# Contracting the ones products of squared rotary halves over 128 rows instead of 64

## The chip, the cores and the metric

The kernel runs on all eight cores of one Trainium2 chip. Each core works on its own share of the tokens and no core waits for another. The metric is the device time of the slowest core in microseconds (us). Executions of a program on all eight cores fall into two states. In the slow state the cores of one die, sometimes of both, show a lower granted TensorE clock than the others (0.83 against 0.99 in one run of the changed kernel, 3170.24 us). The dies are cores 0 to 3 and cores 4 to 7. PE is TensorE (matmuls), PEld its weight loads, DVE is VectorE, ACT is ScalarE, POOL is GpSimd.

## The reference, cut to what matters

```python
# multi-head latent attention, 16 heads, q and k have 128 plain and 64 rotary dimensions
q = apply_rope_tail(rmsnorm(q, q_norm_g[l]), cos, sin)      # norm over all 192
k = apply_rope_tail(rmsnorm(k, k_norm_g[l]), cos, sin)      # k_rope is shared by all heads
y_mla = causal_block_attention(q, k, v) @ w_mla_out[l]
```

The norm needs the sum of 192 squares per token. The kernel keeps dimensions on partitions (rows) and tokens on columns. So it forms these sums on TensorE, as products with a matrix of ones: 128 squared plain dimensions and 64 squared rotary dimensions.

## The kernel before

Two places multiply 64 rows of squares by ones. One is `krstat`, once for each of the 16 key groups of the key/value stage. The other is the unit `QS`, three times for each of the 16 heads of the head stage. `PS[b]` is bank b of the memory into which matmuls write; the latents are the compressed keys and values.

```python
def krstat(g):
    for bb in range(2):                       # one output column each
        mm(PS[BKV][:, 256 + bb:257 + bb], sqkr[0:64, bb * 128:(bb + 1) * 128], ones[0:64, 0:1], True, True,
           [Tsqkr, Tones], [TP[BKV]])
    cp(krss[:, 2 * g:2 * g + 2], PS[BKV][:, 256:258], [TP[BKV]], [Tkrss])

# key/value stage, one turn per key group (cut): 80 latent matmuls of 256 columns into banks 0 to 4,
# first those into bank 0; latents_out reads bank 0 first, on DVE
latents(g); squares(g + 2); kvstat(g); latents_out(g); xstat(g + 2); krstat(g)

def QS(t):
    off, n = QT[t]                            # n = 348, 348, 344
    p = fbank()
    mm(PS[p][:, 0:n], ones, sqn[:, 0:n], True, False, [Tones, Tsqn], [TP[p]])
    mm(PS[p][:, 0:n], ones[0:64, :], sqr[0:64, 0:n], False, True, [Tones, Tsqr], [TP[p]])
    rsq(rsqh[:, 0:n], PS[p][:, 0:n], 192.0, [TP[p]], [Trsqh])        # ACT: Ln, Exp
    ...                                                              # DVE: normalised q

# head stage, per key block (cut): scores, exponential, mask, product with v, running sums
mm(PS[b][:, o:o + n], Kn[hb][:, ks], Qn[hb][:, 128 + lo:128 + hi], True, False, ...)
mm(PS[b][:, o:o + n], krope[:, ks], Qr[hb][:, 128 + lo:128 + hi], False, True, ...)
act(PT[:, x, a:912], psum[:, z + a:z + 912], AF.Exp, ...)            # ACT
tt(PT[:, x, a:a + w], PT[:, x, a:a + w], mask[:, r, 0:w], ALU.mult, ...)                    # DVE, w = 130
mm(PS[b][:, o:o + hi - lo], Vh[hb][:, kb, :], PT[:, x, lo:hi], kb == 0, kb == last, ...)
tt(acc[:, z, a:912], acc[:, z, a:912], PT[:, x, a:912], ALU.add, ...)                       # DVE
```

The program orders each engine's instructions once, when it is built, by a modelled clock. On the chip every engine runs its own list in order and waits on semaphores.

Of the kernel before, what the change touches and what calls it, by code (L numbers as in the profile page):

```python
# [13 lines left out]
PE, ACT, DVE, POOL, SP = "tensor", "scalar", "vector", "gpsimd", "sync"  # L14
# [275 lines left out]
def build_program():  # L290
# [20 lines left out]
    PS = [psum[:, 512 * i:512 * i + 512] for i in range(8)]  # L311
    TP = [T("ps%d" % i, excl=True) for i in range(8)]
    S = Sched(nc)
# [58 lines left out]
    def width(ap):  # L372
        n = 1
        for d in ap.shape[1:]:
            n *= d
        return n

    def mm(out, lhsT, rhs, start, stop, reads, writes):
        S.add(PE, lambda e: e.matmul(out, lhsT=lhsT, rhs=rhs, start=start, stop=stop), reads, writes,  # L379
              cost=max(width(rhs) / 2400.0, 0.055) + 0.003)  # L380
# [9 lines left out]
    def stt(out, in0, scalar, in1, op0, op1, reads, writes):  # L390
        S.add(DVE, lambda e: e.scalar_tensor_tensor(out=out, in0=in0, scalar=scalar, in1=in1, op0=op0, op1=op1),  # L391
              reads, writes, cost=dcost(out, in0, in1))

    def tt(out, in0, in1, op, reads, writes):
        S.add(DVE, lambda e: e.tensor_tensor(out=out, in0=in0, in1=in1, op=op), reads, writes,  # L395
              cost=dcost(out, in0, in1))

    def ts(out, in0, s1, s2, op0, op1, reads, writes):
        c = dcost(out, in0)
        if s2 is None:  # L400
            S.add(DVE, lambda e: e.tensor_scalar(out=out, in0=in0, scalar1=s1, scalar2=None, op0=op0), reads, writes,  # L401
                  cost=c)
        else:
            S.add(DVE, lambda e: e.tensor_scalar(out=out, in0=in0, scalar1=s1, scalar2=s2, op0=op0, op1=op1),  # L404
                  reads, writes, cost=c)

    def cp(out, in_, reads, writes):
        S.add(DVE, lambda e: e.tensor_copy(out=out, in_=in_), reads, writes, cost=dcost(out, in_))  # L408
# [4 lines left out]
    def rsq(out, ssq, n, reads, writes):  # L413

        act(out, ssq, AF.Ln, reads, writes, scale=1.0 / n, bias=EPS)
        act(out, out, AF.Exp, writes, writes, scale=-0.5)
# [4 lines left out]
    ones, Tones = P0.tile([128], BF16, "ones")  # L421
# [102 lines left out]
    sqkr, Tsqkr = P1.tile([GW], BF16, "sqkr")  # L524
# [33 lines left out]

    S.add(DVE, lambda e: e.memset(ones, 1.0), writes=[Tones])  # L559
    S.add(DVE, lambda e: e.memset(krope[64:128, :], 0.0), writes=Tkr)  # L560
    INV2PI = 1.0 / (2.0 * math.pi)
    C1 = 6.28125
    C2 = 2.0 * math.pi - 6.28125
# [5 lines left out]
    for which, dst, Tdst in ((0, tS, TtS), (1, tC, TtC)):  # L569
        if which == 0:  # L570
            ts(rq, ang, INV2PI, None, ALU.mult, None, [Tang], [Trq])
        else:
            ts(rq, ang, INV2PI, 0.25, ALU.mult, ALU.add, [Tang], [Trq])
        cp(rn, rq, [Trq], [Trn])
# [24 lines left out]
    BST, BKV = 6, 5  # L599
# [46 lines left out]

    def krstat(g):
        for bb in range(2):
            mm(PS[BKV][:, 256 + bb:257 + bb], sqkr[0:64, bb * 128:(bb + 1) * 128], ones[0:64, 0:1], True, True,
               [Tsqkr, Tones], [TP[BKV]])  # L650
        cp(krss[:, 2 * g:2 * g + 2], PS[BKV][:, 256:258], [TP[BKV]], [Tkrss])

# [33 lines left out]
    for g in range(NG):  # L686
        if g + 1 < NG:
            make_u(g + 1)
        if g + 3 < NG:
            xload(g + 3)  # L690
        latents(g)
        if g + 2 < NG:
            squares(g + 2)
        kvstat(g)
        latents_out(g)
        if g + 2 < NG:
            xstat(g + 2)
        krstat(g)
        if g == 2:
            halo()  # L700
# [13 lines left out]
    def bank(n=5):  # L714
        b = bk[0] % n
        bk[0] += 1
        return b

    pend = []
    for i in range(6):  # L720
        wv, Tw = wget(("qlat", i))
        for t, (off, n) in enumerate(T3):
            p = bank()
# [43 lines left out]
    sqr, Tsqr = P4.tile([348], BF16, "sqr")  # L767
# [22 lines left out]
    Tgd = [T("gd%d" % i) for i in range(8)]  # L790
    for i_ in range(2):
        S.add(DVE, lambda e, i_=i_: e.memset(Qr[i_][64:128, :], 0.0), writes=[TQr[i_]])  # L792


    class Unit:
# [14 lines left out]
    def fbank():  # L810
        return cur[0]
# [66 lines left out]
    def prologue_units(h):  # L878
# [66 lines left out]
        def QS(t):  # L945
            off, n = QT[t]
            p = fbank()
            mm(PS[p][:, 0:n], ones, sqn[:, 0:n], True, False, [Tones, Tsqn], [TP[p]])
            mm(PS[p][:, 0:n], ones[0:64, :], sqr[0:64, 0:n], False, True, [Tones, Tsqr], [TP[p]])
            rsq(rsqh[:, 0:n], PS[p][:, 0:n], 192.0, [TP[p]], [Trsqh])  # L950

            stt(Qn[hb][:, off:off + n], qraw[:, 0:n], gqe, rsqh[:, 0:n], ALU.mult, ALU.mult,
                [Tqraw, Tgqe, Trsqh], [TQn[hb]])
            tt(Qr[hb][0:64, off:off + n], qr_[0:64, 0:n], rsqh[0:64, 0:n], ALU.mult, [Tqr_, Trsqh], [TQr[hb]])
# [24 lines left out]
        for t in range(3):  # L979
            qq += [Unit(U("q", QN, t), 0.87, ok=okk), Unit(U("q", QR, t), 0.87),  # L980
                   Unit(U("q", QS, t), 0.3, need=[Tsqn, Tsqr], strict=True)]
# [302 lines left out]
    while any(s.units for s in streams):  # L1284
# [19 lines left out]
        if best is None:  # L1304
            n = sum(len(x.pend) for x in streams)
# [17 lines left out]
    for c in range(16):  # L1323
        for key, dst, Td, bo in (("ga", sga, Tsga, 0), ("gb", sgb, Tsgb, 16)):
            w, Tw = wget((key, c))
            for t, (off, n) in enumerate(T3):
                p = bank(8)
# [36 lines left out]
    for c in range(16):  # L1364
        w, Tw = wget(("wo", c))
        for t, (off, n) in enumerate(T3):
            p = bank()
# [199 lines left out]
```

## Time and profile before

| | before |
|---|---|
| time, median of 4 runs | 2769.61 us (2767.91 to 2771.78) |
| matmuls busy, of the span | 95% |
| loads of 64 rows, of all weight loads | 80 of 18,722 |
| excess time at the 48 QS places | 9.8 us |
| period of a key group, median of 15 | 12.92 us |

Groups by form, core 1: weight loads and matmuls of 64 rows. After the bar stand busy us and mean ns of one, then idle us before them and what ended it.

```profile
L379 PEld LDWEIGHTS ps<-arena 128*128 128x128 bf16 x18642 | 1644.6, 98 | 1076.0 <-issue 232.6
L379 PEld LDWEIGHTS ps<-arena 64*128 64x128 bf16 x80 | 6.4, 93 | 24.2 <-issue 24.2
...
L379 PE MATMUL ps<-arena 64*128 64x348 bf16 x32 | 10.2, 318 | 0.0
L379 PE MATMUL ps<-arena 64*128 64x344 bf16 x16 | 5.1, 317 | 0.0
L379 PE MATMUL ps<-arena 64*128 64x1 bf16 x32 | 3.0, 160 | 9.3 <-ACT arena L384 9.3
```

A load of 64 rows takes about as long as one of 128 rows (93 and 98 ns). The idle time before them differs. Of the 24.2 us, 13.3 us stand before the 16 `krstat` pairs, which wait for ACT; 10.9 us stand before the 48 QS loads, 0.23 us each, against 0.06 us before a load of 128 rows.

The timeline around one QS, same core: start us, duration us, engine and instruction.

```profile
442.48 1.39 PE L379 MATMUL ps<-arena 128*128 128x390 bf16 x9
442.81 0.10 PEld L379 LDWEIGHTS ps<-arena 128*128 128x128 bf16 x1
443.21 0.09 PEld L379 LDWEIGHTS ps<-arena 64*128 64x128 bf16 x1 [0.30 <-issue]
443.46 0.28 PEld L379 LDWEIGHTS ps<-arena 128*128 128x128 bf16 x5 [0.16 <-issue]
```

The 64-row load is not pulled ahead of the running matmul as loads usually are. It comes at 443.21, and the next 128-row load comes a quarter of a microsecond later. The single matmuls start at 442.976 (128 rows), 443.218 (64 rows) and 443.469 (128 rows). These are steps of 242 and 251 ns, where 348 columns take 147 ns in a stream.

Worked out from the trace:

- **Excess** of a matmul: its start minus its predecessor's start, minus the predecessor's pace (columns/2.4 + 2.5 ns). That pace comes out of the trace of before, core 1: the median steps after 128, 256, 348, 390 and 512 columns are 56, 109, 147, 165 and 216 ns, where the formula gives 55.8, 109.2, 147.5, 165.0 and 215.8. It is sorted into QS places, places with a semaphore wait for DVE or ACT, and others, and averaged over the six cores of each run whose matmul records are complete.
- **Length of the head stage**: from weight load 2044 to weight load 9100, counted from 0 (the order of instructions is the same in both kernels, and weight-load records are complete; in e2 the same two loads), mean of eight cores. Where a 3.4 us window at half the granted clock fell into it (steps of 427 ns instead of 216 after 512 columns), half of that window is taken off. Most cores of one run then agree to 0.2 us, all to 0.5 us. The slowest core's time doesn't resolve this well: one core's start and end move by several us between runs.

### The profile page before, as it was taken

The numbers are of one execution on the slowest core, as the hardware profiler recorded it, in microseconds if no ns is written. First come the engines' busy times: TensorE is split into PE (matmuls) and PEld (weight loads), VectorE is DVE, ScalarE is ACT, GpSimd is POOL, SyncE is SP. The second block draws the span as 40 slices with busy tenths as digits, with TensorE's granted clock in tenths as the row PEclk, the third lists the DMA queues.
The fourth block names the chain that finished last, engine by engine and source line by source line (L and its number), as shares of the span: only waits on it lengthen the run. The fifth ranks groups of instructions, "written<-read, shape, count | busy, mean of one in ns | idle before, by whom it ended". The sixth has DMA issues, their size and how long they took to land.

```text
span 2770.5 us, 51821 instructions; the slowest of 8 cores (2758.7 to 2770.5 us)
## 1 busy us (share of the span) xinstructions
PE 2624.4 (95%) x18612; PEld 1652.4 (60%) x18722; DVE 1637.5 (59%) x3248; ACT 891.9 (32%) x1598; POOL 172.3 (6%) x300
## 2 busy tenths in 40 slices
PE   3899899999999999999999999999999999999997
PEld 2777555565565555555666666666646646655653
DVE  5774477878887888886111112247727745754762
ACT  3553366656656666664111112320000000000000
POOL 0000000000000000000000000001111011111100
PEclk9999899999999999999999999999999999999999
DMA  9552302020212020215444447444454444444445
GB/s 239 162 171 45 59 18 41 15 41 15 47 18 45 15 41 15 34 42 123 76 72 80 73 75 175 97 73 74 69 83 77 72 74 84 74 69 81 76 87 142
DMA packets 67113, 205.65 MB, mean 74 GB/s; under 512 B 7600, under 2 KB 7856, under 8 KB 66736
## 3 DMA queue, kind: packets, MB, share of 16 engines
q0 software_dynamic: 42624, 135.94, 29.7%
q1 hardware_dynamic: 24240, 66.38, 7.3%
q8 instruction: 157, 2.57, 0.4%
q14 instruction: 92, 0.75, 0.1%
HBM read 321.34 MB, written 14.78 MB: 121 GB/s over the span
## 4 chain that ended last, share of the span: by engine, by line
PE 80%; DVE 6%; issue 5%; ACT 4%; DMA 3%; SPq 1%; DVEq 0%; ACTq 0%; POOLq 0%
PE ps L379 80%; ACT arena L384 4%; DVE arena L395 3%; DMA outT<-arena 2%; DVE arena L391 2%; DVE arena L408 1%; DMA arena<-arena 1%; SPq L411 0%; DVE arena L401 0%; DMA arena<-wall 0%; DVEq L183 0%; ACTq L183 0%; DVE arena L404 0%; DVE arena L560 0%; DVE arena L792 0%
## 5 line engine op out<-in xcount | busy, mean ns | idle before, releaser
L379 PE MATMUL ps<-arena 128*128 128x390 bf16 (+10 forms) x18612 | 2624.4, 299 | 133.4 <-ACT arena L384 81.7
L379 PEld LDWEIGHTS ps<-arena 128*128 128x128 bf16 x18722 | 1652.4, 98 | 1104.9 <-issue 263.3
L395 DVE TENSOR_TENSOR arena<-ps,arena 128x390 f32<-128x390 f32 (+6 forms) x760 | 380.5, 508 | 830.8 <-PE ps L379 716.4
L395 DVE TENSOR_TENSOR arena<-arena 128x512 bf16<-128x512 bf16 (+20 forms) x1458 | 625.6, 474 | 95.6 <-ACT arena L384 69.2
L384 ACT ACTIVATE arena<-ps,arena 128x128 bf16<-128x128 f32 (+10 forms) x672 | 436.2, 672 | 478.0 <-PE ps L379 433.7
L384 ACT ACTIVATE arena<-arena 128x390 bf16<-128x390 f32 (+11 forms) x374 | 227.6, 636 | 898.7 <-DVE arena L391 788.5
L391 DVE SCALAR_TENSOR_TENSOR arena<-arena 128x256 bf16<-128x256 f32 (+8 forms) x583 | 419.7, 755 | 90.2 <-ACT arena L384 67.4
L384 ACT ACTIVATE arena<-ps 128x512 bf16<-128x512 f32 (+13 forms) x547 | 248.5, 472 | 375.3 <-PE ps L379 371.3
L411 POOL DMA_DIRECT2D arena<-wall x294 | 170.9, 582 | 2562.1 <-PE ps L379 2327.7
L408 DVE CAST arena<-ps 128x512 bf16<-128x512 f32 x128 | 87.9, 687 | 45.8 <-PE ps L379 44.4
L404 DVE TENSOR_SCALAR arena<-arena 128x1024 f32<-128x1024 f32 (+1 forms) x90 | 72.3, 803 | 2.6 <-ACT arena L384 2.5
L391 DVE SCALAR_TENSOR_TENSOR arena<-ps,arena 128x256 bf16<-128x256 f32 x64 | 26.5, 476 | 48.8 <-ACT arena L384 48.8
L408 DVE COPY arena<-ps 128x456 f32<-128x456 f32 (+2 forms) x64 | 27.1, 424 | 1.4 <-DVE arena L395 0.5
L401 DVE TENSOR_SCALAR arena<-arena 128x390 f32<-128x390 f32 (+7 forms) x36 | 20.5, 570 | 7.9 <-DMA arena<-arena 5.4
L384 ACT ACT_TABLE_LOAD x5 | 6.4, 1283 | 33.7 <-DVE arena L401 15.5
L395 DVE TENSOR_TENSOR arena<-arena,ps 128x390 bf16<-128x390 f32 (+1 forms) x24 | 12.3, 511 | 2.4 <-PE ps L379 1.5
L408 DVE COPY arena<-arena 128x6 f32<-128x6 f32 (+2 forms) x32 | 9.4, 293 | 2.0
L560 DVE MEMSET arena<- 64x4096 bf16 x1 | 3.5, 3472 | 0.9 <-issue 0.9
L408 DVE CAST arena<-arena 128x1028 f32<-128x1028 int32 (+1 forms) x5 | 3.5, 697 | 0.4
L792 DVE MEMSET arena<- 64x1040 bf16 x2 | 1.9, 925 | 0.4 <-issue 0.4
L559 DVE MEMSET arena<- 128x128 bf16 x1 | 0.2, 165 | 1.2 <-PEq L291 1.2
L411 POOL DMA_DIRECT2D arena<-wkvin x1 | 0.7, 664 | 0.9 <-POOLq L291 0.9
(5 smaller groups left out, 0.9 us busy)
## 6 DMA issues: line engine op xcount, KB each, us to landing
arena<-wall POOLq DMA_DIRECT2D x182, 512.0 KB, 5.8
arena<-xg SPq DMA_DIRECT2D x64, 512.0 KB, 5.2
arena<-wall POOLq DMA_DIRECT2D x64, 352.0 KB, 4.5
arena<-xo SPq DMA_DIRECT2D x16, 520.0 KB, 24.7
arena<-wall POOLq DMA_DIRECT2D x32, 256.0 KB, 3.8
outT<-arena SPq DMA_DIRECT2D x32, 256.0 KB, 3.0
arena<-wall POOLq DMA_DIRECT2D x16, 384.0 KB, 5.1
att_d<-arena SPq DMA_DIRECT2D x16, 260.0 KB, 2.1
```

Source lines behind the costliest of these rows:

```text
L379: S.add(PE, lambda e: e.matmul(out, lhsT=lhsT, rhs=rhs, start=start, stop=stop), reads, writes, cost=max(width(rhs) / 2400.0, 0.055) + 0.003)
L384: S.add(ACT, lambda e: e.activation(out=out, in_=in_, func=func, **kw), reads, writes, cost=c)
L391: S.add(DVE, lambda e: e.scalar_tensor_tensor(out=out, in0=in0, scalar=scalar, in1=in1, op0=op0, op1=op1), reads, writes, cost=dcost(out, ...
L395: S.add(DVE, lambda e: e.tensor_tensor(out=out, in0=in0, in1=in1, op=op), reads, writes, cost=dcost(out, in0, in1))
L401: S.add(DVE, lambda e: e.tensor_scalar(out=out, in0=in0, scalar1=s1, scalar2=None, op0=op0), reads, writes, cost=c)
L404: S.add(DVE, lambda e: e.tensor_scalar(out=out, in0=in0, scalar1=s1, scalar2=s2, op0=op0, op1=op1), reads, writes, cost=c)
L408: S.add(DVE, lambda e: e.tensor_copy(out=out, in_=in_), reads, writes, cost=dcost(out, in_))
L411: S.add(eng, lambda e: e.dma_start(out=out, in_=in_), reads=reads, writes=writes, chan=chan, cost=2.0)
L559: S.add(DVE, lambda e: e.memset(ones, 1.0), writes=[Tones])
L560: S.add(DVE, lambda e: e.memset(krope[64:128, :], 0.0), writes=Tkr)
L792: S.add(DVE, lambda e, i_=i_: e.memset(Qr[i_][64:128, :], 0.0), writes=[TQr[i_]])
```

## The change

The upper 64 rows of the squares are set to zero once, and both products then contract over all 128 rows. The result is the same and no product of fewer rows is left. The cost is two small memsets.

```diff
     S.add(DVE, lambda e: e.memset(krope[64:128, :], 0.0), writes=Tkr)
+    S.add(DVE, lambda e: e.memset(sqkr[64:128, :], 0.0), writes=[Tsqkr])
...
-            mm(PS[BKV][:, 256 + bb:257 + bb], sqkr[0:64, bb * 128:(bb + 1) * 128], ones[0:64, 0:1], True, True,
+            mm(PS[BKV][:, 256 + bb:257 + bb], sqkr[:, bb * 128:(bb + 1) * 128], ones[:, 0:1], True, True,
...
+    S.add(DVE, lambda e: e.memset(sqr[64:128, :], 0.0), writes=[Tsqr])
...
-            mm(PS[p][:, 0:n], ones[0:64, :], sqr[0:64, 0:n], False, True, [Tones, Tsqr], [TP[p]])
+            mm(PS[p][:, 0:n], ones, sqr[:, 0:n], False, True, [Tones, Tsqr], [TP[p]])
```

## The prediction

> **What bounds the kernel.** The page of before: matmuls busy 95% of the 2770.5 us span, 80% of the chain of waits. By stretches (busy time in windows): key/value stage, 70 to 300 us, 209 of 230 us; head stage, 345 to 1500 us, 1111 of 1155 us, DVE at 70%, ACT at 54%; the rest (1600 to 2760 us) 1148 of 1160 us. TensorE bounds it; in the head stage its waits are 37 us, for ACT 18 and DVE 17.
>
> **What the change touches.** 80 weight loads of 64 rows (groups by form): 48 second products of QS (64x348/344, three per head), and 32 one-column products of krstat (two per key group). All other 18,642 loads have 128 rows, so each QS, and each krstat pair, switches the array to 64 rows and back. The Trainium skill, "TensorEngine Tiling (Array Packing)", Key Properties, says a change of tiling mode drains TensorE. The trace agrees: in a stream a load is issued one matmul ahead; at a QS the 64-row load comes only some 240 ns after the 128-row matmul began, the matmul starts 243 ns after it where 147 ns (348/2.4 + 2.5) is the pace, and the next 128-row matmul 250 ns later instead of 147. The excess is 95 + 103 ns at almost all 48 places. Matmul and load themselves take the same at 64 and 128 rows (318 and 310 ns; 93 and 98 ns).
>
> **Removed, QS.** 48 x 198 ns = 9.5 us of TensorE time. None hides a wait: the squares were written over 1 us before each. It lies where TensorE is 96% busy; some turns into waits for ACT and DVE: I take 85 to 95%, 8.5 us.
>
> **Removed, krstat: nearly nothing.** The next matmul starts 295 ns after the pair, which looks like a drain of 270 ns x 14. But it waits: the latents' first matmul needs bank 0, freed by a DVE product. Semaphore times in one group: DVE's update at 132.395 us, matmul at 132.531; 136 ns, as after every wait. Before the pair, TensorE waits for ACT's square. Both drains lie under waits. The 12.92 us period of a key group stays (at most 0.05 us less).
>
> **Added.** Two memsets on DVE: sqkr 64x256, about 0.3 us at the start, on the chain there (the 64x4096 memset took 3.47 us, 0.85 ns a column); sqr 64x348, about 0.4 us with its gap near 320 us, where DVE's two 0.93 us memsets are on the chain. Together +0.7 us. They also shift the modelled clock by which the program orders the head stage's units; the order may change in places: +-3 us.
>
> **Sum.** -8.5 + 0.7 = about -8 us: 2762 us, 0.3% faster. Range 2755 to 2769. Over 2% faster: 1%; within 2%: 98%; slower: 1%.
>
> **What would show it.** By form, no 64-row matmul is left and 18,722 loads have 128 rows; a QS's second matmul and its follower start about 147 ns apart; period of a key group still 12.92 us, with a matmul 136 ns after DVE's update; the third memset lengthens the wait at 320 us by 0.3 to 0.4 us; the head stage 7 to 10 us shorter, everything after it unchanged.
>
> **What would make it wrong.** The drain's cost not in the row count but in the swap of stationary operand or the accumulation into one bank; head stage bound by ACT's and DVE's chain, so that 9.5 us become waits; a different order of units worth over 3 us; the krstat drain setting the period after all (3.8 us more).

## More of the kernel before

Busy time in windows, core 1 of the kernel before. The first column is the window from the span's start in us. The second is its length. Then follow the busy us of each engine (with the number of instructions), the granted clock, the DMA share and GB/s. The rows are the key/value stage, most of the head stage, and the rest.

```profile
70.00:300.00 230.00, 209.11 (x1766) 166.24 (x1764) 137.16 (x348) 109.27 (x217) 3.70 (x7) 1.00 0.42 120
330.00:1215.00 885.00, 850.18 (x6919) 517.09 (x6918) 718.08 (x1738) 558.02 (x1008) 24.28 (x46) 1.00 0.16 29
1600.00:2740.00 1140.00, 1132.54 (x7060) 686.87 (x7059) 595.96 (x773) 111.33 (x172) 111.22 (x181) 1.00 0.49 86
```

In the head stage TensorE is busy 96% of the time, but DVE is busy 81% (718 of 885 us).

## The result, and the profile after

Ratios are the mean time of one kernel's fast runs over that of the other's in the same timing rounds. The profiled execution of each kernel, the first in its list, seems to be left out of them: for e15 the means without it divide to 0.9983, with it to 0.9987.

| | before | changed |
|---|---|---|
| first comparison | 2769.61 us | fast runs 2769.76 and 2766.61 us; ratio 0.9994 (95%: 0.997 to 1.0018) |
| second comparison, run e15 | 4 fast runs, mean 2772.9 us (2771.4 with the profiled one) | 4 fast runs, mean 2768.1 us (2767.8 with the profiled one); ratio 0.9982 (0.9966 to 0.9998) |
| length of the head stage | 898.1 us | 893.5 us |
| excess at the 48 QS places | 9.8 us | 1.2 us |
| excess at waits for DVE / for ACT, head stage | 32.9 / 32.6 us | 37.0 / 33.0 us |
| period of a key group | 12.92 us | 12.92 us |

The first comparison had two further runs of the changed kernel, slow (2858.42 and 3170.24 us), which lift its plain median to 2814.09 us. They say nothing of the change. By the two ratios the time is 0.06% and 0.18% lower, the first within the noise. The stages tell more than the total: the head stage is 4.5 us shorter (898.1 - 893.5, before rounding).

The order of the instructions on every engine is unchanged; only the two memsets are new. So each weight load of the changed kernel can be set against the same one of before.

Groups by form and the timeline of the same QS, core 1 of the changed kernel.

```profile
L379 PEld LDWEIGHTS ps<-arena 128*128 128x128 bf16 x18722 | 1653.0, 98 | 1094.8 <-issue 249.6
```

```profile
441.92 1.34 PE L379 MATMUL ps<-arena 128*128 128x390 bf16 x10
442.26 0.89 PEld L379 LDWEIGHTS ps<-arena 128*128 128x128 bf16 x8
```

No 64-row load is left, and the loads run through without a gap. The matmuls start at 442.585, 442.732 and 442.879: 147 ns each, twice.

Busy time in windows, core 1 of the changed kernel, the same three windows:

```profile
70.00:300.00 230.00, 209.15 (x1762) 165.99 (x1761) 137.61 (x349) 108.89 (x216) 3.70 (x7) 1.00 0.42 120
330.00:1215.00 885.00, 847.88 (x6972) 521.53 (x6970) 718.26 (x1742) 558.50 (x1012) 24.28 (x46) 1.00 0.15 29
1600.00:2740.00 1140.00, 1133.14 (x7049) 686.12 (x7047) 596.87 (x775) 110.72 (x171) 110.36 (x180) 1.00 0.49 86
```

In the same 885 us of the head stage 53 more matmuls start (6972 against 6919), and TensorE is busy a little less. Each matmul is booked with a modelled length (318 ns for those of QS), longer than the 242 and 251 ns steps, so "busy" counted the drains as work.

The waits of TensorE in the head stage, 330 to 1215 us, core 1: first before, then changed. Columns: total us, times, longest us.

```profile
PE ps L379 <- ACT arena L384: 17.3, 45, 1.6
PE ps L379 <- DVE arena L395: 9.0, 24, 1.1
PE ps L379 <- DVE arena L408: 3.5, 7, 1.2
```

```profile
PE ps L379 <- ACT arena L384: 17.2, 44, 1.6
PE ps L379 <- DVE arena L395: 10.3, 28, 1.3
PE ps L379 <- DVE arena L408: 3.9, 8, 1.2
```

The waits for ACT stay and the waits for DVE grow. This view leaves out gaps under 150 ns. The measure of excess, which has them all, shows +4.1 us for DVE (32.9 to 37.0) and +0.4 us for ACT. That is where the gain went: 8.6 us gained at the QS places, 4.5 us taken back at waits. What is left, 4.1 us by this sum, agrees with the 4.5 us of shortening to a few tenths.

### The profile page after: what moved, and what is told of

The parts are those of the page before. It is cut to its first block, busy times and chain, and to the rows that moved or that the text cites. A ratio compares the mean times of both kernels' runs of the same rounds, so it can differ in the third digit from the quotient of the medians.

```text
span 2768.0 us, 51934 instructions; the slowest of 8 cores (2754.8 to 2768.0 us)
## 1 busy us (share of the span) xinstructions
PE 2625.8 (95%) x18722; PEld 1653.8 (60%) x18722; DVE 1636.8 (59%) x3250; ACT 891.6 (32%) x1598; POOL 171.9 (6%) x300
## 4 chain that ended last, share of the span: by engine, by line
PE 80%; DVE 6%; issue 5%; ACT 4%; DMA 4%; SPq 0%; DVEq 0%; ACTq 0%; POOL 0%; POOLq 0%
PE ps L379 80%; ACT arena L384 4%; DVE arena L395 4%; DMA outT<-arena 2%; DMA arena<-xg 1%; DVE arena L391 1%; DVE arena L408 1%; DMA arena<-wall 1%; SPq L411 0%; DVEq L183 0%; ACTq L183 0%; DVE arena L401 0%; DVE arena L793 0%; DVE arena L404 0%; POOL arena L411 0%
## 5 line engine op out<-in xcount | busy, mean ns | idle before, releaser
L379 PE MATMUL ps<-arena 128*128 128x390 bf16 (+8 forms) x18722 | 2625.8, 300 | 130.1 <-ACT arena L384 82.6
L384 ACT ACT_TABLE_LOAD x5 | 6.4, 1283 | 35.0 <-DVE arena L401 16.5
```

The source lines that it names most:

```text
L379: S.add(PE, lambda e: e.matmul(out, lhsT=lhsT, rhs=rhs, start=start, stop=stop), reads, writes, cost=max(width(rhs) / 2400.0, 0.055) + 0.003)
L384: S.add(ACT, lambda e: e.activation(out=out, in_=in_, func=func, **kw), reads, writes, cost=c)
```

## The experiments

The twelve runs are e2 to e9 and e12 to e15. "Before" and "changed" name the two kernels. e2 to e9 and e12 have one fast execution each: 2779.16, 2763.82, 2756.59, 2747.53, 2774.43, 2768.26, 2759.26, 2740.17 and 2769.22 us in the order of their names. Beside e2 to e9 the kernel before ran slow only, so their totals have no fast base; the stages are compared instead.

### Is it the switch of the row count, and what does one cost?

**e2, twice as many switches.** The pair of QS is cut into two halves of the columns.

```diff
-            mm(PS[p][:, 0:n], ones, sqn[:, 0:n], True, False, ...)
-            mm(PS[p][:, 0:n], ones[0:64, :], sqr[0:64, 0:n], False, True, ...)
+            for a, b in ((0, n // 2), (n // 2, n)):          # modelled cost kept, so the order is kept
+                mm(PS[p][:, a:b], ones, sqn[:, a:b], True, False, ...)
+                mm(PS[p][:, a:b], ones[0:64, :], sqr[0:64, a:b], False, True, ...)
```

> The kernel before with each QS pair cut into two column halves (128 rows, 64 rows, 128 rows, 64 rows): the same columns, four switches of row count where there were two. Drain at each switch: the excess over the pace of TensorE's matmuls, summed over the 48 QS places, doubles from 9.8 us to about 19 us (about 98 ns a switch); the head stage (from the 2044th to the 9100th weight load) grows by 4 to 9 us, less than the 9.5 us if ACT's and DVE's waits take some of it in. Rival, a fixed cost per visit (a wait on the squares, the first use of the bank): excess stays near 10 us, head stage within 1 us.

Measured: excess at QS 19.0 us (before 9.8), head stage 906.4 us (before 898.1). The timeline of the same QS, core 1:

```profile
444.65 0.77 PE L949 MATMUL ps<-arena 128*128 128x174 bf16 x4
444.82 0.45 PEld L949 LDWEIGHTS ps<-arena 64*128 64x128 bf16 x3 [0.23 <-issue]
```

The five starts from 444.650 on are 170, 178, 181 and 177 ns apart, where 174 columns take 75 ns in a stream. So each switch costs 95 to 106 ns, about as with 348 columns (92 to 104 ns), and the rival of one cost per visit falls. Of the 9.2 us added, 8.3 us arrived in the head stage.

**e3, 96 rows.** The changed kernel with the second QS product over 96 rows.

```diff
-            mm(PS[p][:, 0:n], ones, sqr[:, 0:n], False, True, ...)
+            mm(PS[p][:, 0:n], ones[0:96, :], sqr[0:96, 0:n], False, True, ...)
```

> The changed kernel with the second QS product over 96 rows instead of 128 (rows 64 to 95 are zero). Tiling-mode theory: 96 rows don't fit a half of the array, so it runs in the mode of 128 rows and no drain is seen: excess at the QS places 1.2 us as in the changed kernel, follower 147 ns later. Rival, any row count that differs from its neighbours' drains: excess 9.8 us as before, 240 to 250 ns steps.

Measured: excess at QS 1.4 us, head stage 893.7 us, as in the changed kernel. Groups by form, core 1:

```profile
L379 PE MATMUL ps<-arena 96*128 96x348 bf16 x32 | 10.2, 318 | 0.0
L379 PE MATMUL ps<-arena 96*128 96x344 bf16 x16 | 5.0, 311 | 0.0
```

96 rows stand between products of 128 rows without any drain: in the trace the starts are 147 and 150 ns apart. It is not a differing number of rows that costs. Nor is it the swap of the stationary operand or the accumulation into one bank, the prediction's other suspects: e3 and the changed kernel keep both. 64 rows are something else for TensorE than 96 or 128, as a tiling mode would be.

### Where did the rest of the gain go?

The theory: DVE, at 81%, can't follow a faster TensorE. The rival: the gain is lost to ACT, or to the fixed order, however much DVE has to do. The two kernels of each pair below have the same lightened DVE work and differ only by the change itself. Their outputs are wrong, which doesn't matter for the times. The modelled costs are kept, and with them the order.

**e4 and e5, running sums a quarter wide** (e4 on before, e5 on changed).

```diff
-            tt(acc[:, z, a:912], acc[:, z, a:912], PT[:, x, a:912], ALU.add, ...)
+            m = a + (912 - a) // 4 // 2 * 2
+            tt(acc[:, z, a:m], acc[:, z, a:m], PT[:, x, a:m], ALU.add, ...)     # modelled cost kept
```

> Wrong result on purpose: the kernel before with the running sums of the softmax on DVE cut to the first quarter of their columns, order of all instructions kept. A base for e5. Excess at the QS places 9.8 us as before; waits for DVE in the head stage below 33 us.

> The same cut of DVE's sums in the changed kernel. If DVE's work is what takes back 4 to 5 us of the 8.6 us that the QS places gain, then with DVE lightened the head stage of this run is 7.5 to 9 us shorter than that of e4. Rival, the gain is lost to ACT or to the fixed order of instructions whatever DVE does: 3 to 5 us shorter, as between the two kernels uncut.

**e8 and e9, still less on DVE** (e8 on before, e9 on changed).

```diff
-            tt(acc[:, z, a:912], acc[:, z, a:912], PT[:, x, a:912], ALU.add, ...)
+            tt(acc[:, z, a:a + 8], acc[:, z, a:a + 8], PT[:, x, a:a + 8], ALU.add, ...)
-            tt(sqk[:, ct % 2, :], kn, kn, ALU.mult, ...)                 # 512 columns
+            tt(sqk[:, ct % 2, 0:ws], kn[:, 0:ws], kn[:, 0:ws], ...)      # 128 from the second head on
-            ts / stt / stt of the gated conv over 130 columns a block
+            the same over 32 columns from the second channel group on
```

The conv edit narrows three instructions.

> Wrong result on purpose: the kernel before with still less on DVE (running sums 8 columns wide, two conv products and the squares of the keys a quarter wide, order kept). A base for e9. Excess at the QS places about 9.5 us; waits for DVE below the 19 us of e4.

> The same lightening in the changed kernel. Between e4 and e5 6.5 us of 8.7 us arrived. If DVE's load takes back the rest too, this run's head stage is 7.5 to 8.7 us shorter than that of e8. Rival, what is still taken back is the latency of the chain from a score matmul over ACT's exponential and DVE's mask to the next product, whatever DVE's load: 6 to 7 us shorter again.

| pair (64 rows, 128 rows) | DVE busy, 330 to 1215 us, core 1 of the 64-row kernel | gained at QS | head stage | shorter by | share |
|---|---|---|---|---|---|
| before, changed | 718.1 us | 8.6 us | 898.1, 893.5 us | 4.5 us | 53% |
| e4, e5 | 579.4 us | 8.7 us | 884.9, 878.4 us | 6.5 us | 74% |
| e8, e9 | 499.8 us | 8.8 us | 882.3, 875.1 us | 7.2 us | 81% |

The share is the last length over the gain at QS. Two further pairs with DVE's full work, e6/e7 and e12/e13 below, differ by 4.4 and 4.2 us in the head stage, as before and changed do. In the bases e4 and e8 the excess at QS is 9.1 us (9.8 and about 9.5 were expected), and the waits for DVE are about 19 and 16.5 us, as expected; the waits for ACT rise from 32.6 us to 36.4 us in both. The windows of DVE's work in e4 and e8, core 1:

```profile
330.00:1215.00 885.00, 857.21 (x7041) 527.82 (x7039) 579.39 (x1753) 560.83 (x1019) 24.28 (x46) 1.00 0.15 29
330.00:1215.00 885.00, 858.95 (x7075) 530.26 (x7074) 499.82 (x1757) 562.33 (x1021) 24.28 (x46) 1.00 0.15 29
```

Waits for DVE, e4 and then e5, core 1, 330 to 1215 us:

```profile
PE ps L379 <- DVE arena L395: 4.9, 10, 1.1
PE ps L379 <- DVE arena L408: 1.9, 3, 1.0
```

```profile
PE ps L379 <- DVE arena L395: 5.0, 10, 1.1
PE ps L379 <- DVE arena L408: 2.3, 4, 1.0
```

They hardly grow any more. By excess the waits for DVE rise by 1.9 us from e4 to e5, where they rose by 4.1 us uncut.

Both measured differences lie between the ranges that the two theories had claimed. DVE's load is shown to be a cause: lightening it brings 2.0 us, then 2.6 us, of the missing 4.1 us (8.6 - 4.5) back. It is not shown to be the whole cause. With DVE at 56% some 1.6 us are still taken back, 0.6 us of it at waits for ACT. The latency from a score product over the exponential and the mask to the next product would fit. It was not tested alone.

The traces show one thing more, which DVE's share does not explain: the loss is uneven. Between weight loads 3050 and 5150 (452 to 725 us) the 13 QS places gain 2.4 us and the stretch becomes only 0.15 us shorter. Between 7100 and 9100 (972 to 1226 us) 13 places gain 2.6 us, and the whole 2.6 us arrive. The pairs e6/e7 and e12/e13 repeat this (0.04 and 0.17 us; 2.6 and 2.4 us). Yet DVE is as busy in the one as in the other (82% and 81%), and the waits for DVE are longer in the second (9.6 and 12.1 us of excess in before, places that wait for ACT as well included). With DVE lightened the first stretch gets 1.15 us (e4/e5) and 1.4 us (e8/e9) shorter. So neither DVE's share nor the sum of the waits for it tells where a gain is lost. What does, no run here shows.

### Do the one-column products of krstat drain too?

**e6 and e7, another bank for the first latent matmuls** (e6 on before, e7 on changed).

```diff
+    lb = lambda g, m: 7 if m == 0 and g % 2 == 0 else m
-            mm(PS[m][:, 0:GW], wkv[:, k, ...], uc[ub][:, k, :], ..., [TP[m]])
+            b = lb(g, m)
+            mm(PS[b][:, 0:GW], wkv[:, k, ...], uc[ub][:, k, :], ..., [TP[b]])
```

> The kernel before (64 rows) with the latents' first accumulator in bank 7 at even key groups, bank 0 at odd ones, so the matmul after krstat no longer waits for DVE to free bank 0. Theory: the 295 ns after the krstat pair were set by that wait and, equally long, by the drain; with the wait gone the drain alone is left, about 270 to 295 ns, and the period of a key group stays at 12.9 us (12.85 to 12.92). Rival, one-column products drain nothing: the follower comes about 25 to 30 ns after the pair and the period falls to about 12.65 us.

> The same alternation of banks in the changed kernel (128 rows). Theory: now neither wait nor drain is there; the follower starts 25 to 60 ns after the pair and the period of a key group is 0.2 to 0.27 us shorter than in e6, 3 to 4 us over the stage. Rival, the period is set by another wait: e6 and e7 have the same period.

Measured: the period became longer, 13.05 to 13.24 us in both, and the load after the pair came 111 ns after the pair's second load in e6 and 93 ns in e7 (288 ns in before and changed). The follower, the next matmul, started 101 ns after the pair in both, where 270 to 295 ns and 25 to 60 ns had been expected. Both claims about the period were wrong. The trace shows why. In before, one wait on bank 0 also told TensorE that all earlier DVE work was done. Without it each of the first 16 latent matmuls has a semaphore wait of its own, for its slice of the inputs, and these matmuls start 126 ns apart (median) instead of 109. So the experiment replaced one wait by sixteen. Still, it shows that no drain of 270 ns stands behind the pair.

**e12, the same with one early wait** (on before, 64 rows).

```diff
             mm(PS[BKV][:, 256 + bb:257 + bb], sqkr[0:64, ...], ones[0:64, 0:1], True, True,
-               [Tsqkr, Tones], [TP[BKV]])
+               [Tsqkr, Tones] + (Tuc[(g + 1) % 2] if g + 1 < NG else []), [TP[BKV]])
```

> As e6 (64 rows, alternating bank), and the krstat product also waits for the next group's normalised inputs, so the latents' matmuls wait for nothing of DVE. In e6 each of the first 16 had a wait of its own (126 ns apart instead of 108), which one wait on bank 0 had covered before. Theory: a switch back to 128 rows costs about 98 ns from the start of the last one-column product, whatever its width, so the follower comes 95 to 105 ns after it, and the period falls from 12.92 to 12.70 to 12.75 us. Rival, the 270 ns drain that the prediction took as an upper bound: follower at 270 to 295 ns, period 12.92 us.

Measured: the follower starts 92 to 93 ns after the last one-column product, just under the 95 to 105 ns expected, and the period is 12.84 us. The period fell by 0.08 us, less than half of what was expected, because the pair itself now has two waits one after the other: its load comes 181 ns after the start of the instruction in which TensorE waits for ACT, where it came 77 ns after it in before.

**e13, the same on the changed kernel**, with the memsets of `Qr` and `sqr` on POOL.

```diff
-        S.add(DVE, lambda e, i_=i_: e.memset(Qr[i_][64:128, :], 0.0), writes=[TQr[i_]])
-    S.add(DVE, lambda e: e.memset(sqr[64:128, :], 0.0), writes=[Tsqr])
+        S.add(POOL, lambda e, i_=i_: e.memset(Qr[i_][64:128, :], 0.0), writes=[TQr[i_]])
+    S.add(POOL, lambda e: e.memset(sqr[64:128, :], 0.0), writes=[Tsqr])
```

> The changed kernel with the bank alternation and early wait of e12, and with the memsets of the upper halves of Qr and sqr on POOL. Follower of the krstat pair at 25 to 30 ns (no switch), period 12.62 to 12.68 us, 0.07 us less than e12; key stage 3 to 4 us shorter than in the changed kernel, the wait before the head stage about 2 us shorter, head stage as in the changed kernel (893.6 us). Time 0.15 to 0.3% below the changed kernel. Rival, the stage is bound elsewhere: period within 0.05 us of 12.92.

Measured: the follower starts 25 ns after the last one-column product, and the period is 12.76 us, 0.08 us less than in e12; 12.62 to 12.68 us had been expected. The switch behind a one-column product therefore costs 67 ns (92 - 25), not 270; the step after the follower is 10 ns longer in e12 too (120 against 109 ns), which makes up the 0.08 us. The one-column krstat pair in the timelines, core 1 of e12 and of e13:

```profile
161.34 1.68 PEld L379 LDWEIGHTS ps<-arena 64*128 64x128 bf16 x17 [0.81 <-issue]
161.37 1.82 PE L379 MATMUL ps<-arena 64*128 64x1 bf16 x16 [0.56 <-ACT arena L384]
```

```profile
157.40 1.60 PEld L379 LDWEIGHTS ps<-arena 128*128 128x128 bf16 x17 [0.81 <-issue]
157.43 1.74 PE L379 MATMUL ps<-arena 128*128 128x1 bf16 x16 [0.56 <-ACT arena L384]
```

The same 16 matmuls take 0.08 us less, and the same idle time for ACT stands before both. The wait ahead of the head stage is 1.6 us shorter than in the changed kernel (median from the 1950th to the 2044th load 23.1 against 24.7 us). From the fourth to the last krstat pair the key/value stage is 2.1 us shorter (149.4 against 151.5 us), not the 3 to 4 us expected. The head stage is the same (893.9 us). The ratio to before is 0.9966 (0.9946 to 0.9985). Against the changed kernel in the same rounds it is 2762.8/2767.8 = 0.9982, the means of four and five fast runs with the profiled ones, for which no interval was worked out.

### Can the gain be had back by moving work from DVE?

**e14, e13 with the squares of the keys on ACT.**

```diff
-            tt(sqk[:, ct % 2, :], kn, kn, ALU.mult, [TKn[hb][ct]], [Tsqk[ct % 2]])
+            act(sqk[:, ct % 2, :], PS[p], AF.Square, [TP[p]], [Tsqk[ct % 2]])
```

> e13 with the 128 squares of the keys on ACT, from PSUM, instead of on DVE (the program's modelled clock then orders the head stage anew). If DVE's load is what takes back the gain in the head stage, waits for DVE fall well under 37 us and the head stage becomes 5 to 15 us shorter than in e13. Rival, ACT is as tight as DVE, or the new order is worse: head stage as long or longer.

This one is inconclusive. The modelled clock ordered the head stage anew, and the profile fell in the slow state. On its undisturbed die, from the 1950th to the 11,200th weight load, it took 1226.0 us on average against 1228.7 us in e13 (four cores against eight; half-clock windows of 3.4 us corrected), so about 3 us less and not the 5 to 15 us expected. The ratio of fast runs to before is 0.9986 (0.992 to 1.0051), one of them at 2791 us. It is not shown to be faster than e13.

**e15, the changed kernel again,** for a tighter interval.

> The changed kernel once more, timed in the same rounds as e13 and e14. Ratio to the kernel before 0.997 to 0.9995: the head stage's 4.5 us and nothing else. Rival, no gain at all: ratio 1.000 with the interval on both sides and a head stage of 898 us.

Measured: ratio 0.9982 (0.9966 to 0.9998), head stage 893.6 us. It repeats the first trace to 0.1 us in the head stage. The interval just excludes 1. It should not be leaned on: with the profiled executions (2765.45 us for before, 2766.83 us for e15) the means differ by 3.6 us, where the fast runs of either kernel scatter over more than 8 us. The shorter head stage is the firm result.

## Why the prediction was right or wrong

- **What bounds the kernel: right, but not far enough.** TensorE is busy 96% in the head stage. DVE stands there as 70%, over a window to 1500 us that runs past the end of the stage (1226 us); inside the stage, 330 to 1215 us, it is busy 81%.
- **The drain: right.** The prediction read 95 + 103 ns from the trace. The change removed 8.6 of 9.8 us there, e2 doubled it to 19.0 us, and e3 tied it to 64 rows rather than to any row count that differs from its neighbours'. The Trainium skill, "TensorEngine Tiling (Array Packing)", Key Properties, states that a change of tiling mode drains TensorE. These runs agree with it (92 to 106 ns a switch at the QS places), if 64 rows are such a mode, which no run shows directly.
- **The share that would arrive: wrong, and this is the step that failed.** The prediction took "85 to 95%, 8.5 us". Measured: 4.5 us of 8.6 us, 53%. The term was mis-sized, not its sign. A head stage with 37 us of waits looked as if it had little room to take time back, though the excess, which has the short gaps too, puts the waits at 65.5 us (32.9 + 32.6). Every place where TensorE already waits is a place where a gain made since the last wait can be lost. e4, e5, e8 and e9 show that DVE's load takes back at least 2.6 of the 4.1 us; the rest stays open.
- **krstat nearly nothing: right, wait included.** The period stayed at 12.92 us, and the matmul behind the pair waited for DVE as predicted. The prediction left open how large the drain under that wait is, up to the 270 ns that "looks like a drain". With the wait away, e12 and e13 show 67 ns.
- **The memsets: right.** The one of 64x256 took 0.27 us at the start. The one of 64x348 lengthened DVE's stretch ahead of the head stage from 2.30 to 2.69 us, on the chain. Order of units: unchanged, so the 3 us kept for it were not needed.
- **The sum.** Predicted about -8 us. With the measured term it is -4.5 + 0.7 = -3.8 us, 0.14%. The two comparisons (0.06% and 0.18% faster, each with an interval about 0.3 to 0.5 points wide) contain that. The two fast runs of the first comparison averaged 2768.2 us, inside the range by its upper edge and 6 us above the point; one of them, 2769.76 us, lies outside it. That the total fell into the range owes something to luck: two of the four runs of the kernel before, 2767.91 and 2768.84 us, lie in it as well.
- **Left open.** One half-clock window of 3.4 us fell into the head stage near 475 us on five of eight cores of the changed kernel's first profile and on two of before, at about 1.7 us each. No run here shows what decides it.

## What to carry to other kernels

Before booking a saving on the engine that looks like the bound, look at the second engine inside the stage concerned: here half of what TensorE saved came back, mostly as waits for an engine at 81%. But take a high share as a warning only: in the last 254 us of the stage the whole saving arrived at the same 81%. The test in the other direction would have misled here: adding 9.2 us of drains lengthened the stage by 8.3 us, while removing 8.6 us shortened it by only 4.5 us. And a wait that looks redundant may cover others: taking it away in e6 put sixteen waits in its place and made the loop longer.

## What the Trainium skill lacked or had wrong

- "TensorEngine Tiling (Array Packing)", Key Properties, gives no time for the drain of a mode switch. Here it was 92 to 106 ns a switch with 174 or 348 columns, and 67 ns behind a one-column product.
- The same page, Tiling Modes, lists no row tiling (128 rows) and row tiles of 64 and of 32 rows, and doesn't say what a product over another number of rows runs as. Here 96 rows ran between 128-row products without a drain (e3: 1.4 us of excess against 9.8 us).
- "TensorE: Matmul & The Clock Gate", LDWEIGHTS, says that a load's time does not depend on its rows. The trace agrees (93 ns with 64 rows, 98 ns with 128). It doesn't say that a load is not pulled ahead across a switch between 128 and 64 rows: here the 64-row load of a QS came only 238 ns after the matmul before it had started (443.214 against 442.976 us), with 0.23 us idle before it against 0.06 us before a load of 128 rows.
- None of the pages gives the price of a semaphore wait on TensorE that is already satisfied. In e6 a wait before each 256-column matmul made the pace 126 ns instead of 109 (median), and in e12 a second wait ahead of the pair, for work that DVE had done 3.8 us earlier, cost 104 ns (181 - 77).
